# A hybrid conv/mLSTM decoder block on one core: the gates' rows moved by steps, and another order and other engines for the last block's output

## The chip, the cores and the metric

The kernel runs on one core of a Trainium2 chip. The metric is the device time of one execution in microseconds, as the median of several runs. The profile is one further execution, with its own time; the span in it goes from the first to the last instruction.

## What is computed

One decoder block on 512 rows of width 1024 in float32, cut here to what matters:

```python
hn = rmsnorm(x, g_mix)
xa, ba, ca, za, q, k, v, o, zb, ig, fg, ga, gb = split(hn @ w_in)
ya = (ba * causal_short_conv(ca * xa, conv_w, conv_b) * silu(za)) @ w_a_out
hb = mlstm_chunkwise(q, k, v, ig + b_i, fg + b_f)        # 4 heads; log gates, running maximum
yb = (sigmoid(o) * rmsnorm(hb, g_head) * silu(zb)) @ w_b_out
x = x + (sigmoid(ga) * ya + sigmoid(gb) * yb) @ w_o
gate = sigmoid(rmsnorm(x, g_ple) @ w_ple_gate)
x = x + gate * (p @ w_ple)
return rmsnorm(x, g_final)
```

The two input and forget gates are one value per row and head. From them come, per head, cumulative sums, running maxima and the exponents' offsets, here called the gates' rows.

## The kernel before, in words

Every float32 matmul is made of three matmuls on rounded halves: `mm3` (L194 to L198) takes a high half `whi` (rounded on ACT, L144) and a low half `wlo` (what is left, on DVE, L145) of the weights, and two such halves of the other side. `split_half` makes the halves of one half of a weight block, and issues on POOL's queue the loads that add another weight block into the raw one (L151). The raw blocks, four at a time, are loaded over SP's queue (L127).

Most products are `strassen`: seven products of two steps each, a step being twelve matmuls on PE, with the results put together on ACT (`s`, `v`, L307) and DVE (`c`, L311). Its left sides are half-sums of the normalised input, `hs`, rounded by `left` on ACT (L596) and DVE (L598) beside the first such product.

The order of each engine's instructions is that in which the program is written. `step` is called after a step's matmuls and calls `tick`: it resumes the small generators that work beside the matmuls, first the new ones, then makes one piece of a weight split, then resumes the others. A `yield` in a generator is therefore one step of PE. SP's queue alone is ordered by the scheduler.

Around the change three generators matter:

- `gate_rows` (L620 to L679) makes the gates' rows on four partitions, in a tile `rows`: Abs, Exp and Ln on ACT (L629, L630, L636), sums, running maxima and `negm`, `mrow` on DVE (L665, L669). 14 transposes on PE (L674, L676) put them into `ptc`, DVE copies that to `colsb` (L678), ACT makes `enm` (L679). DVE also splits `negm` into `nmr` (L666, L668), which a matmul spreads over the partitions (`pnb`, L744).
- `scores` (L735 on) makes one head's score tiles. Head 0 has its q and k from DRAM: they are loaded into `qk_raw` (L795) once the start's tiles, `rows` among them, are given back, and `cut` (L203, L204) splits them.
- at the end, the product for the gate on `p @ w_ple` is made for columns 0 to 511 in a `block_tm` and for the others by `last_part`, in row blocks t of 128, the last one in two quarters. `gated` takes sigmoid on ACT (L1027), a product and a sum into `xr` on DVE (L1028, L1029) and the sum of squares on ACT (L1030). `power` starts 1/sqrt on POOL, `final` does a Newton step and writes the two halves of the output on DVE (L1064) from `xg`, the product of `xr` and `g_final` that `weighted` made on POOL (L1068); SP issues the stores (L1065).

Of the kernel before, what the change touches and what calls it, by code (L numbers as in the profile page):

```python
# [9 lines left out]
F32 = mybir.dt.float32  # L10
F32R = mybir.dt.float32r
AF = mybir.ActivationFunctionType
ALU = mybir.AluOpType

P = 128
S = 512
NT = S // P
# [19 lines left out]
def hybrid_block(ctx, tc, x, p, g_mix, w_in, conv_w, conv_b, w_a_out, b_gates, g_head,  # L37
# [152 lines left out]
    def drain():  # L190
        while active or fresh:
            tick()
# [55 lines left out]
    def temp(tag, name=None, dt=F32):  # L248

        return tp.tile([P, S], dt, name=name or tag, tag=tag, bufs={"c": 3}.get(tag, 2))  # L250
# [369 lines left out]
    def gate_rows():  # L620
# [3 lines left out]
        yield  # L624
# [6 lines left out]
        yield  # L631
# [13 lines left out]
        yield  # L645
# [20 lines left out]
        dve.tensor_copy(nmr[0:NH], negm)  # L666
        yield
        dve.tensor_tensor(nmr[32:32 + NH], negm, nmr[0:NH].bitcast(F32), ALU.subtract)  # L668
# [6 lines left out]
        for t in range(NT):  # L675
            pe.transpose(ptc[:, 40 + 4 * t:44 + 4 * t], mrow[:, t * P:(t + 1) * P], ident[:NH, :NH])  # L676
        yield
        dve.tensor_copy(colsb, ptc[:, :56])  # L678
        act.activation(enm.rearrange("p t h -> p (t h)"), colsb[:, 40:], AF.Exp)  # L679
# [55 lines left out]
    def scores(h, qk, pr, pp, done, raw):  # L735

        if raw is not None:
            yield
            for m in range(4):
                cut(qk[0][:, m, :], qk[1][:, m, :], raw[:, m, :])  # L740
                if m == 1:
                    yield
# [278 lines left out]
    xg = mp.tile([P, NT, D], F32, name="xg", tag="m")  # L1021

    def gated(ps, t, c, i):

        sl = xr[:, t, c]
        g, sq = (temp(u)[:, :c.stop - c.start] for u in "ec")
        act.activation(g, ps, AF.Sigmoid, scale=er[:, t:t + 1])  # L1027
        dve.tensor_tensor(g, g, ple[:, t, c], ALU.mult)  # L1028
        dve.tensor_tensor(sl, sl, g, ALU.add)  # L1029
        act.activation(sq, sl, AF.Square, accum_out=fss[:, t, i:i + 1])  # L1030

    def gate_embedding(t, ps):
        gated(ps, t, half[0], 0)
        yield

    block_tm([(h2, 0), (h2, HC)], gate_embedding)
    drain()

    base = ep.tile([P, NT], F32, name="base")
    dve.tensor_scalar(base, fss[:, :, 0], 1.0 / D, EPS, ALU.mult, ALU.add)  # L1040
# [10 lines left out]

    def power(t, i):
        a, r, _ = (u[:, t:t + 1] for u in etmp)
        dve.tensor_scalar(a, fss[:, t, i:i + 1], 1.0 / D, base[:, t:t + 1], ALU.mult, ALU.add)
        pool.tensor_tensor(r, a, mhalf[:, :1], ALU.pow)

    def final(t):

        a, r, e = (u[:, t:t + 1] for u in etmp)
        dve.scalar_tensor_tensor(e, r, a, r, ALU.mult, ALU.mult)  # L1060
        dve.tensor_scalar(e, e, -0.5, 1.5, ALU.mult, ALU.add)
        for n in range(2):
            y = temp("sv"[n], "y")
            dve.tensor_scalar(y, xg[:, t, half[n]], r, e, ALU.mult, ALU.mult)  # L1064
            nc.sync.dma_start(out[0, t * P:(t + 1) * P, half[n]], y)  # L1065

    def weighted(t, c):
        pool.tensor_tensor(xg[:, t, c], xr[:, t, c], gfin[:, c], ALU.mult)  # L1068

    pss = [bank(t) for t in range(NT)]  # L1070
    for t in range(2):
        last_part(t, [0], 0, CW, pss[t])
    for t in range(3):
        last_part(t, [1] if t < 2 else [0, 1], 0, CW, pss[t])
# [3 lines left out]
    for t in range(NT):  # L1078
        weighted(t, half[0])
    q = [slice(CW, CW + CW // 2), slice(CW + CW // 2, D)]  # L1080
    gated(pss[0], 0, half[1], 1)
    power(0, 1)
    weighted(0, half[1])
    gated(pss[1], 1, half[1], 1)
    final(0)
    power(1, 1)
    weighted(1, half[1])
    final(1)
    gated(pss[2], 2, half[1], 1)
    power(2, 1)  # L1090
    weighted(2, half[1])
    gated(pss[3][:, :CW // 2], 3, q[0], 1)
    weighted(3, q[0])
    final(2)
    gated(psl[:, :CW // 2], 3, q[1], 2)
    dve.tensor_scalar(base[:, 3:4], fss[:, 3, 1:2], 1.0 / D, base[:, 3:4], ALU.mult, ALU.add)
    weighted(3, q[1])
    power(3, 2)
    final(3)
# [23 lines left out]
```

## Time and profile before

| what | us |
|---|---|
| median of 3 runs | 889.19 (888.02 to 889.53) |
| the profiled execution, its own time | 886.59 |
| its span | 884.8 |
| PE busy | 863.3 (98%) |
| DVE busy | 568.3 (64%) |
| ACT busy | 438.6 (50%) |
| POOL busy | 240.6 (27%) |
| TensorE's mean granted clock | 0.994 of full speed |

The span is shorter than the execution's time by 1.8 us, which lie around it. An engine's busy time is a sum over its instructions; neighbouring ones overlap by up to 0.1 us, so busy time and distance of starts differ a little. A row of the timeline shows in brackets how long the engine had been idle and what ended that. Matmuls overlap: what one costs is the distance of starts.

### The profile page before, as it was taken

The numbers are of one execution on the slowest core, as the hardware profiler recorded it, in microseconds if no ns is written. First come the engines' busy times: TensorE is split into PE (matmuls) and PEld (weight loads), VectorE is DVE, ScalarE is ACT, GpSimd is POOL, SyncE is SP. The second block draws the span as 40 slices with busy tenths as digits, with TensorE's granted clock in tenths as the row PEclk, the third lists the DMA queues.
The fourth block names the chain that finished last, engine by engine and source line by source line (L and its number), as shares of the span: only waits on it lengthen the run. The fifth ranks groups of instructions, "written<-read, shape, count | busy, mean of one in ns | idle before, by whom it ended". The sixth has DMA issues, their size and how long they took to land.

```text
span 884.8 us, 11787 instructions
## 1 busy us (share of the span) xinstructions
PE 863.3 (98%) x4555; PEld 740.3 (84%) x4555; DVE 568.3 (64%) x744; ACT 438.6 (50%) x639; POOL 240.6 (27%) x236
## 2 busy tenths in 40 slices
PE   7999999999999999999999999999999999999995
PEld 6887688888888888888887999999988888888874
DVE  4759586775675667856884678788872323554446
ACT  6477575546545665546575454645431111224442
POOL 4642422332232313223422534243310100000023
PEclk9999999999999999999999999999999999999998
DMA  9799986969846887887869989898996674422002
GB/s 297 252 215 244 253 192 145 234 196 243 206 142 180 198 192 170 237 218 170 216 163 270 236 182 182 181 179 199 210 412 236 199 258 140 134 96 96 0 1 95
DMA packets 97031, 169.64 MB, mean 192 GB/s; under 512 B 6032, under 2 KB 43984, under 8 KB 94544
## 3 DMA queue, kind: packets, MB, share of 16 engines
q0 software_dynamic: 35616, 76.03, 41.2%
q1 hardware_dynamic: 61360, 92.87, 31.9%
q8 instruction: 35, 0.57, 0.3%
q14 instruction: 20, 0.16, 0.1%
HBM read 148.96 MB, written 19.92 MB: 191 GB/s over the span
## 4 chain that ended last, share of the span: by engine, by line
PE 84%; DVE 5%; DMA 4%; ACT 2%; issue 2%; POOL 1%; SPq 0%; POOLq 0%; DVEq 0%; ACTq 0%
PE mm L198 25%; PE mm L197 25%; PE mm L196 25%; DMA wraw<-in_w_in 2%; DVE wlo L145 2%; DMA qk_raw<-qk_d 1%; PE pv L196 1%; PE pv L197 1%; PE pv L198 1%; DVE xr L1029 1%; ACT whi L144 1%; PE ptk L960 1%; PE pty L729 1%; DVE e L1028 1%; DMA pin<-in_p 1%
## 5 line engine op out<-in xcount | busy, mean ns | idle before, releaser
L145 DVE TENSOR_TENSOR wlo<-wraw,whi 128x1024 fp32r<-128x1024 f32 x222 | 283.4, 1281 | 156.5 <-ACT whi L144 155.6
L144 ACT ACTIVATE whi<-wraw 128x1024 fp32r<-128x1024 f32 x224 | 234.5, 1054 | 138.7 <-PE mm L198 98.3
L151 POOL DMA_DIRECT2D wraw<-in_w_in x110 | 138.3, 1446 | 269.5 <-DVE wlo L145 199.1
L196 PE MATMUL mm<-hn_hi,whi 128*128 128x256 f32 (+1 forms) x320 | 105.1, 328 | 0.0
L198 PE MATMUL mm<-hn_hi,wlo 128*128 128x256 f32 (+1 forms) x320 | 104.4, 326 | 0.2 <-POOL wlo L145 0.2
L197 PE MATMUL mm<-hn_lo,whi 128*128 128x256 f32 (+1 forms) x320 | 104.2, 326 | 0.0
L196 PE MATMUL mm<-whi,hs 128*128 128x512 f32 x256 | 100.1, 391 | 0.4 <-ACT v L307 0.3
L197 PE MATMUL mm<-wlo,hs 128*128 128x512 f32 x256 | 99.9, 390 | 0.3 <-DVE wlo L145 0.3
L198 PE MATMUL mm<-whi,hs 128*128 128x512 f32 x256 | 99.7, 389 | 0.0
L307 ACT ACTIVATE s<-mm 128x512 f32<-128x512 f32 x72 | 42.9, 596 | 85.3 <-PE mm L198 85.1
L196 PE MATMUL mm<-whi,hn_hi 128*128 128x512 f32 x192 | 76.2, 397 | 1.0 <-ACT whi L144 0.7
L197 PE MATMUL mm<-wlo,hn_hi 128*128 128x512 f32 x192 | 75.8, 395 | 0.8 <-DVE wlo L145 0.8
L198 PE MATMUL mm<-whi,hn_lo 128*128 128x512 f32 x192 | 75.3, 392 | 0.0
L198 PE MATMUL mm<-hs,wlo 128*128 128x256 f32 x256 | 72.5, 283 | 0.3 <-DVE wlo L145 0.3
L196 PE MATMUL mm<-hs,whi 128*128 128x256 f32 x256 | 72.4, 283 | 0.0
L197 PE MATMUL mm<-hs,whi 128*128 128x256 f32 x256 | 72.4, 283 | 0.0
L198 PEld LDWEIGHTS mm<-hn_hi,wlo 128*128 128x128 f32 x320 | 60.9, 190 | 5.7 <-POOL wlo L145 0.8
L197 PEld LDWEIGHTS mm<-hn_lo,whi 128*128 128x128 f32 x320 | 60.9, 190 | 4.7
L196 PEld LDWEIGHTS mm<-hn_hi,whi 128*128 128x128 f32 x320 | 60.9, 190 | 4.6
L196 PEld LDWEIGHTS mm<-whi,hs 128*128 128x128 f32 x256 | 48.1, 188 | 10.8 <-ACT v L307 0.7
L197 PEld LDWEIGHTS mm<-wlo,hs 128*128 128x128 f32 x256 | 48.1, 188 | 10.3 <-DVE wlo L145 0.8
L198 PEld LDWEIGHTS mm<-whi,hs 128*128 128x128 f32 x256 | 48.1, 188 | 10.0
(257 smaller groups left out, 1662.8 us busy)
## 6 DMA issues: line engine op xcount, KB each, us to landing
wraw<-in_w_in SPq DMA_DIRECT2D x32, 1024.0 KB, 6.3
wraw<-in_w_in POOLq DMA_DIRECT2D x62, 512.0 KB, 7.6
wraw<-in_w_in SPq DMA_DIRECT2D x48, 512.0 KB, 4.8
wraw<-in_w_in POOLq DMA_DIRECT2D x48, 256.0 KB, 5.9
yt_d<-yc POOLq DMA_DIRECT2D x8, 1024.0 KB, 8.4
wraw<-in_w_b_out SPq DMA_DIRECT2D x8, 1024.0 KB, 12.3
yt<-yt_d POOLq DMA_DIRECT2D x8, 1024.0 KB, 10.6
wraw<-in_w_a_out SPq DMA_DIRECT2D x4, 1024.0 KB, 9.8
```

The source lines that it names most:

```text
L144: act.activation(hi, t, AF.Copy)
L145: (e_lo or dve).tensor_tensor(lo, t, hi.bitcast(F32), ALU.subtract)
L151: nc.gpsimd.dma_start(raws[to][:, ks, cs], src[:, ks, :], accum_op=ALU.add)
L196: pe.matmul(ps, lhsT=a[0], rhs=b[0], start=first, stop=False, **kw)
L197: pe.matmul(ps, lhsT=a[0], rhs=b[1], start=False, stop=False, **kw)
L198: pe.matmul(ps, lhsT=a[1], rhs=b[0], start=False, stop=last, **kw)
L307: act.activation(to[i], src, AF.Copy, scale=scale)
L729: pe.transpose(pts[v][:, t * P:(t + 1) * P], y[:, t, v * P:(v + 1) * P], ident)
L960: pe.transpose(pts[k][:, t * P:(t + 1) * P], src[:, t, k * P:(k + 1) * P], ident)
L1028: dve.tensor_tensor(g, g, ple[:, t, c], ALU.mult)
L1029: dve.tensor_tensor(sl, sl, g, ALU.add)
```

## The change

Four yields of `gate_rows` go, and four are put ahead of `enm`, which so stays at its step: every part of the rows comes one to four steps earlier. `mrow` is made with `negm`, a step ahead of the transposes, and the split of `negm` into `nmr` comes behind them. `scores` waits one step more before it cuts head 0's q and k. At the end, the Square and the product with `g_final` of a row block's first half come a step after its sigmoid; the drain stands behind the first two parts of the last block and `base` behind all of them; POOL multiplies only the first half of the columns, the other is multiplied on DVE in the output's own instruction; a new `fs` holds the product of the two factors of the scale; block 2's output stands behind the last sum, and one half of block 3's output is made on ACT.

```diff
--- before.py
+++ after.py
@@ -621,7 +621,6 @@
         for g, dst in enumerate((li, lf)):
             act.activation(dst, psg[64 + 32 * g:64 + 32 * g + NH, :], AF.Identity, bias=bg[:, g:g + 1])
         yield
-        yield
         for g, dst in enumerate((li, lf)):
             dve.tensor_tensor(dst, dst, psg[32 * g:32 * g + NH, :], ALU.add)
         yield
@@ -629,7 +628,6 @@
         act.activation(la, lf, AF.Abs)
         act.activation(la, la, AF.Exp, scale=-1.0)
         yield
-        yield
         dve.tensor_scalar(u1, la, 1.0, None, ALU.add)
         dve.scalar_tensor_tensor(off, u1, 1.0, la, ALU.subtract, ALU.subtract)
         yield
@@ -642,7 +640,6 @@
 
         for t in range(NT):
             dve.tensor_tensor_scan(bc[:, t, :], ones[:NH].broadcast_to([NH, P]), lfv[:, t, :], 0.0, ALU.mult, ALU.add)
-        yield
         dve.tensor_tensor(ul0f, li, bcf, ALU.subtract)
         dve.tensor_copy(ul[:, 0, :], ul0[:, 0, :])
         yield
@@ -663,9 +660,6 @@
             if t % 2:
                 yield
         dve.tensor_scalar(negm, mxf, -1.0, None, ALU.mult)
-        dve.tensor_copy(nmr[0:NH], negm)
-        yield
-        dve.tensor_tensor(nmr[32:32 + NH], negm, nmr[0:NH].bitcast(F32), ALU.subtract)
         dve.tensor_tensor(mrow, negm, bcf, ALU.subtract)
         yield
 
@@ -674,8 +668,12 @@
             pe.transpose(ptc[:, 4 * n:4 * n + 4], ul[:, n, :], ident[:NH, :NH])
         for t in range(NT):
             pe.transpose(ptc[:, 40 + 4 * t:44 + 4 * t], mrow[:, t * P:(t + 1) * P], ident[:NH, :NH])
+        dve.tensor_copy(nmr[0:NH], negm)
+        dve.tensor_tensor(nmr[32:32 + NH], negm, nmr[0:NH].bitcast(F32), ALU.subtract)
         yield
         dve.tensor_copy(colsb, ptc[:, :56])
+        for _ in range(4):
+            yield
         act.activation(enm.rearrange("p t h -> p (t h)"), colsb[:, 40:], AF.Exp)
 
     colsb = const.tile([P, 56], F32, name="colsb")
@@ -735,6 +733,7 @@
     def scores(h, qk, pr, pp, done, raw):
 
         if raw is not None:
+            yield
             yield
             for m in range(4):
                 cut(qk[0][:, m, :], qk[1][:, m, :], raw[:, m, :])
@@ -1018,26 +1017,28 @@
 
     active.append(norm_scale())
     fss = ep.tile([P, NT, 4], F32, name="fss")
-    xg = mp.tile([P, NT, D], F32, name="xg", tag="m")
-
-    def gated(ps, t, c, i):
+    xg = mp.tile([P, NT, D], F32, name="xg", tag="m")[:, :, half[0]]
+
+    def gated(ps, t, c):
 
         sl = xr[:, t, c]
-        g, sq = (temp(u)[:, :c.stop - c.start] for u in "ec")
+        g = temp("e")[:, :c.stop - c.start]
         act.activation(g, ps, AF.Sigmoid, scale=er[:, t:t + 1])
         dve.tensor_tensor(g, g, ple[:, t, c], ALU.mult)
         dve.tensor_tensor(sl, sl, g, ALU.add)
-        act.activation(sq, sl, AF.Square, accum_out=fss[:, t, i:i + 1])
+
+    def squares(t, c, i):
+        act.activation(temp("c")[:, :c.stop - c.start], xr[:, t, c], AF.Square, accum_out=fss[:, t, i:i + 1])
 
     def gate_embedding(t, ps):
-        gated(ps, t, half[0], 0)
-        yield
+        gated(ps, t, half[0])
+        yield
+        squares(t, half[0], 0)
+        pool.tensor_tensor(xg[:, t, :], xr[:, t, half[0]], gfin[:, half[0]], ALU.mult)
 
     block_tm([(h2, 0), (h2, HC)], gate_embedding)
-    drain()
 
     base = ep.tile([P, NT], F32, name="base")
-    dve.tensor_scalar(base, fss[:, :, 0], 1.0 / D, EPS, ALU.mult, ALU.add)
     wl = []
 
     def last_part(t, cs, a, b, ps):
@@ -1049,54 +1050,69 @@
                     [u[kt][:, a:b] for u in wl[c]], c == 0 and kt == 0, c == 1 and kt == HC - 1)
             tick()
 
+    fs = ep.tile([P, NT], F32, name="fs")
+
     def power(t, i):
         a, r, _ = (u[:, t:t + 1] for u in etmp)
         dve.tensor_scalar(a, fss[:, t, i:i + 1], 1.0 / D, base[:, t:t + 1], ALU.mult, ALU.add)
         pool.tensor_tensor(r, a, mhalf[:, :1], ALU.pow)
 
-    def final(t):
-
+    def final_scale(t):
         a, r, e = (u[:, t:t + 1] for u in etmp)
         dve.scalar_tensor_tensor(e, r, a, r, ALU.mult, ALU.mult)
         dve.tensor_scalar(e, e, -0.5, 1.5, ALU.mult, ALU.add)
-        for n in range(2):
-            y = temp("sv"[n], "y")
-            dve.tensor_scalar(y, xg[:, t, half[n]], r, e, ALU.mult, ALU.mult)
-            nc.sync.dma_start(out[0, t * P:(t + 1) * P, half[n]], y)
-
-    def weighted(t, c):
-        pool.tensor_tensor(xg[:, t, c], xr[:, t, c], gfin[:, c], ALU.mult)
+        dve.tensor_tensor(fs[:, t:t + 1], r, e, ALU.mult)
+
+    def final(t, n, on_act=False):
+
+        y = temp("sv"[n], "y")
+        f = fs[:, t:t + 1]
+        if n:
+            dve.scalar_tensor_tensor(y, xr[:, t, half[1]], f, gfin[:, half[1]], ALU.mult, ALU.mult)
+        elif on_act:
+            act.activation(y, xg[:, t, :], AF.Copy, scale=f)
+        else:
+            dve.tensor_scalar(y, xg[:, t, :], f, None, ALU.mult)
+        nc.sync.dma_start(out[0, t * P:(t + 1) * P, half[n]], y)
 
     pss = [bank(t) for t in range(NT)]
     for t in range(2):
         last_part(t, [0], 0, CW, pss[t])
+    drain()
     for t in range(3):
         last_part(t, [1] if t < 2 else [0, 1], 0, CW, pss[t])
     psl = ps_x.tile([P, S], F32, name="mml", tag="x")
     last_part(3, [0, 1], 0, CW // 2, pss[3])
     last_part(3, [0, 1], CW // 2, CW, psl)
-    for t in range(NT):
-        weighted(t, half[0])
+    dve.tensor_scalar(base, fss[:, :, 0], 1.0 / D, EPS, ALU.mult, ALU.add)
     q = [slice(CW, CW + CW // 2), slice(CW + CW // 2, D)]
-    gated(pss[0], 0, half[1], 1)
+    gated(pss[0], 0, half[1])
+    squares(0, half[1], 1)
     power(0, 1)
-    weighted(0, half[1])
-    gated(pss[1], 1, half[1], 1)
-    final(0)
+    gated(pss[1], 1, half[1])
+    squares(1, half[1], 1)
     power(1, 1)
-    weighted(1, half[1])
-    final(1)
-    gated(pss[2], 2, half[1], 1)
+    final_scale(0)
+    for n in range(2):
+        final(0, n)
+    final_scale(1)
+    for n in range(2):
+        final(1, n)
+    gated(pss[2], 2, half[1])
+    squares(2, half[1], 1)
     power(2, 1)
-    weighted(2, half[1])
-    gated(pss[3][:, :CW // 2], 3, q[0], 1)
-    weighted(3, q[0])
-    final(2)
-    gated(psl[:, :CW // 2], 3, q[1], 2)
+    gated(pss[3][:, :CW // 2], 3, q[0])
+    squares(3, q[0], 1)
+    final_scale(2)
+    gated(psl[:, :CW // 2], 3, q[1])
+    squares(3, q[1], 2)
     dve.tensor_scalar(base[:, 3:4], fss[:, 3, 1:2], 1.0 / D, base[:, 3:4], ALU.mult, ALU.add)
-    weighted(3, q[1])
+    final(2, 0)
     power(3, 2)
-    final(3)
+    final(2, 1)
+    final_scale(3)
+    final(3, 0, True)
+    final(3, 1)
     close(ep_ctx, mp_ctx, hp_ctx, tp_ctx, mg_ctx)
```

ACT in the gates' stage, before. `rows` at L629 and L630 are Abs and Exp, at L636 Ln; `whi` are high halves of weights, `hs` those of the left sides, `s` results taken from PSUM:

```order
L596 ACTIVATE hs_116<-hsf_448 128x1024
L307 ACTIVATE s<-mm 128x512
L144 ACTIVATE whi_583<-wraw_336 128x1024
L629 ACTIVATE rows<-rows 4x512
L630 ACTIVATE rows<-rows 4x512
L307 ACTIVATE s<-mm 128x512
L144 ACTIVATE whi_608<-wraw_334 128x1024
L596 ACTIVATE hs_122<-hnf 128x1024
L144 ACTIVATE whi_629<-wraw_334 128x1024
L144 ACTIVATE whi_652<-wraw_440 128x1024
L636 ACT_TABLE_LOAD
L636 ACTIVATE rows<-rows 4x512
```

and now:

```order
L628 ACTIVATE rows<-rows 4x512
L629 ACTIVATE rows<-rows 4x512
L596 ACTIVATE hs_116<-hsf_448 128x1024
L307 ACTIVATE s<-mm 128x512
L144 ACTIVATE whi_585<-wraw_336 128x1024
L307 ACTIVATE s<-mm 128x512
L144 ACTIVATE whi_610<-wraw_334 128x1024
L634 ACT_TABLE_LOAD
L634 ACTIVATE rows<-rows 4x512
L596 ACTIVATE hs_122<-hnf 128x1024
L144 ACTIVATE whi_632<-wraw_334 128x1024
```

Abs, Exp and Ln with its table load stand ahead of more of the high halves; Ln, which was behind `whi_652`, is now ahead of `whi_632`, the second half of the block before.

DVE in the same stage at `negm` (L665 before, L662 now) and `mrow` (L669, L663), before:

```order
L311 TENSOR_TENSOR c<-s,v 128x512
L145 TENSOR_TENSOR wlo_844<-wraw_588,whi_843 128x1024
L665 TENSOR_SCALAR rows<-rows 4x512
L666 CAST nmr<-rows 4x512
L145 TENSOR_TENSOR wlo_868<-wraw_588,whi_867 128x1024
L668 TENSOR_TENSOR nmr<-rows,nmr 4x512
L669 TENSOR_TENSOR rows<-rows 4x512
L678 COPY colsb<-ptc 128x56
```

and now:

```order
L659 SCALAR_TENSOR_TENSOR rows<-rows,carry 4x128
L311 TENSOR_TENSOR c<-s,mm 128x512
L145 TENSOR_TENSOR wlo_776<-wraw_338,whi_775 128x1024
L662 TENSOR_SCALAR rows<-rows 4x512
L663 TENSOR_TENSOR rows<-rows 4x512
L311 TENSOR_TENSOR c<-s,mm 128x512
L145 TENSOR_TENSOR wlo_800<-wraw_334,whi_799 128x1024
L671 CAST nmr<-rows 4x512
L672 TENSOR_TENSOR nmr<-rows,nmr 4x512
L311 TENSOR_TENSOR c<-s,v 128x512
L145 TENSOR_TENSOR wlo_839<-wraw_334,whi_838 128x1024
L674 COPY colsb<-ptc 128x56
```

`mrow` follows `negm` at once, ahead of the casts to `nmr`, and two low halves now stand between `mrow` and the copy of `ptc` to `colsb`.

DVE at the program's end, before (`e` and `xr` of the last quarter are rows 2 and 3):

```order
L1064 TENSOR_SCALAR y<-xg,etmp_6827,etmp_6828 128x512 x2
L1028 TENSOR_TENSOR e<-e,ple 128x256
L1029 TENSOR_TENSOR xr<-xr,e 128x256
L1096 TENSOR_SCALAR base<-fss,base 128x1
L1054 TENSOR_SCALAR etmp_6826<-fss,base 128x1
L1060 SCALAR_TENSOR_TENSOR etmp_6828<-etmp_6827,etmp_6826 128x1
L1061 TENSOR_SCALAR etmp_6828<-etmp_6828 128x1
L1064 TENSOR_SCALAR y<-xg,etmp_6827,etmp_6828 128x512 x2
```

and now:

```order
L1027 TENSOR_TENSOR e<-e,ple 128x256
L1028 TENSOR_TENSOR xr<-xr,e 128x256
L1109 TENSOR_SCALAR base<-fss,base 128x1
L1075 TENSOR_SCALAR y<-xg,fs 128x512
L1057 TENSOR_SCALAR etmp_6826<-fss,base 128x1
L1071 SCALAR_TENSOR_TENSOR y<-xr,fs,gfin 128x512
L1062 SCALAR_TENSOR_TENSOR etmp_6828<-etmp_6827,etmp_6826 128x1
L1063 TENSOR_SCALAR etmp_6828<-etmp_6828 128x1
L1064 TENSOR_TENSOR fs<-etmp_6827,etmp_6828 128x1
L1071 SCALAR_TENSOR_TENSOR y<-xr,fs,gfin 128x512
```

Block 2's output (L1075, L1071) stands behind the last sum, one half of it behind block 3's power input; of block 3's output DVE makes one half.

On PE the 14 transposes stand 36 matmuls earlier, `pnb` twelve later and head 0's score tiles twelve later. On SP three of the four loads of `qk_raw` stand ahead of a weight load that they followed. Nothing else is moved on POOL than the products with `g_final`.

## Rows read from the trace of the kernel before

**Rows 1.** PE's waits, whole span: engine, line, waited for: us, times, longest.

```profile
PE ptc L676 <- DVE rows L669: 1.4, 1, 1.4
```

**Rows 2.** Timeline of PE, 77 to 108: start, us, instruction [idle before <-releaser].

```profile
79.42 0.40 PE L197 MATMUL mm<-wlo,hs 128*128 128x512 f32 x1
...
88.78 0.39 PE L198 MATMUL mm<-whi,hn_lo 128*128 128x512 f32 x1
...
91.65 0.72 PE L196 MATMUL mm<-whi,hn_hi 128*128 128x512 f32 x1
...
95.40 0.40 PE L196 MATMUL mm<-whi,hn_hi 128*128 128x512 f32 x1
...
101.32 0.39 PE L198 MATMUL mm<-whi,hn_lo 128*128 128x512 f32 x1
...
104.89 0.39 PE L196 MATMUL sc<-qk 128*128 128x512 f32 x1
...
107.68 0.50 PE L196 MATMUL mm<-whi,hs 128*128 128x512 f32 x1
```

**Rows 3.** Stages: length, busy time of the five engines, PEclk, DMA share, GB/s.

```profile
92.00:95.00 3.00, 3.00 (x8) 2.32 (x8) 1.23 (x1) 1.16 (x2) 3.00 (x4) 0.50 1.14 253
```

**Rows 4.** Timeline of PE, 856 to 875.

```profile
856.72 0.50 PE L196 MATMUL mm<-whi,h 128*128 128x512 f32 x1 [0.45 <-ACT whi L144]
...
857.98 0.50 PE L197 MATMUL mm<-wlo,h 128*128 128x512 f32 x1 [0.76 <-DVE wlo L145]
...
874.44 0.28 PE L198 MATMUL mml<-whi,h 128*128 128x256 f32 x1
```

**Rows 5.** Timeline of ACT, 50 to 61.

```profile
50.08 1.05 ACT L144 ACTIVATE whi<-wraw 128x1024 fp32r<-128x1024 f32 x1
...
53.75 0.61 ACT L629 ACTIVATE rows<-rows 4x512 f32<-4x512 f32 x1
...
60.84 1.28 ACT L636 ACT_TABLE_LOAD   x1 [0.67 <-DVE rows L634]
```

**Rows 6.** Timeline of DVE, 58 to 78.

```profile
58.50 1.23 DVE L145 TENSOR_TENSOR wlo<-wraw,whi 128x1024 fp32r<-128x1024 f32 x1
...
60.08 0.68 DVE L634 SCALAR_TENSOR_TENSOR rows<-rows 4x512 f32<-4x512 f32 x1
...
67.11 1.22 DVE L145 TENSOR_TENSOR wlo<-wraw,whi 128x1024 fp32r<-128x1024 f32 x1 [3.48 <-ACT whi L144]
...
77.95 1.21 DVE L145 TENSOR_TENSOR wlo<-wraw,whi 128x1024 fp32r<-128x1024 f32 x1
```

**Rows 7.** Stages, DVE's instructions on the tile rows alone: length, busy (count), PEclk, DMA.

```profile
58.40:61.00 2.60, 1.09 (x2) 1.00 1.07 243
...
78.00:88.00 10.00, 3.75 (x14) 1.00 0.77 229
```

**Rows 8.** Timeline of ACT, 876 to 877.

```profile
876.44 0.46 ACT L1027 ACTIVATE e<-mml,er 128x256 f32<-128x256 f32 x1
```

**Rows 9.** Timeline of DVE, 864 to 881.

```profile
864.41 0.69 DVE L1028 TENSOR_TENSOR e<-e,ple 128x512 f32<-128x512 f32 x1 [0.36 <-ACT e L1027]
...
877.40 0.41 DVE L1028 TENSOR_TENSOR e<-e,ple 128x256 f32<-128x256 f32 x1
...
878.90 0.21 DVE L1054 TENSOR_SCALAR etmp<-fss,base 128x1 f32<-128x1 f32 x1 [0.51 <-ACT c L1030]
...
880.22 1.00 DVE L1064 TENSOR_SCALAR y<-xg,etmp,etmp 128x512 f32<-128x512 f32 x2
```

**Rows 10.** SP's stores of the output: line, count: ns min/median/max, first and last start.

```profile
L1065 SPq DMA_DIRECT2D out<-y x8: 332/350/373, 867.7 to 881.2; - x8
```

**Rows 11.** Timeline of DVE and POOL, 261 to 865.

```profile
261.28 1.22 DVE L145 TENSOR_TENSOR wlo<-wraw,whi 128x1024 fp32r<-128x1024 f32 x1
...
261.45 1.96 POOL L865 TENSOR_TENSOR cols<-cols,mhalf 128x4 f32<-128x4 f32 x1 [10.83 <-DVE cols L864]
...
864.19 0.55 POOL L1055 TENSOR_TENSOR etmp<-etmp,mhalf 128x1 f32<-128x1 f32 x1 [7.92 <-DVE etmp L1054]
```

## Prediction

> **What bounds the kernel now.** I read the page first: by its part 1 TensorE is busy nearly throughout, so only what PE waits for, what slows it, and what follows its last matmul can be won. The list of PE's waits puts one of the longest, 1.4 us, on the four transposes L676 that need the row `mrow` [rows 1]. PE's timeline shows what that wait costs: the last matmul before the 14 transposes into `ptc` starts at 88.78, the next one at 91.65; from there to 95.40 nine matmuls start 0.42 us apart, while the 26 that follow to 101.32 start 0.23 apart; and the six matmuls of head 0's first score tile take from 104.89 to 107.68 [rows 2]. The table by stages gives the reason of the slow nine: the clock granted was 0.50, the lower of its two levels, 1.2 of 2.4 GHz [rows 3]. Near the end PE stalls twice, for the high and the low half of the last weight block, and its last matmul starts at 874.44 [rows 4], 10.4 us before the span ends.
>
> The sums stand against one execution: 886.59 us, 884.8 of them span. It lies 2.6 below the median of 889.19 and 1.4 below the fastest of the three runs, so I take differences from it and subtract them from 889.19.
>
> **The change part by part.**
>
> *The wait at ptc.* PE reaches the transposes three steps (36 matmuls) earlier, but `mrow` is made four steps earlier and a whole step ahead of them. From 88.78 to 91.65 is 2.87: 0.23 for the matmul, the rest transposes and wait. The transposes stay. I take −1.4, the listed wait [rows 1]; 0 if `mrow` is late again.
>
> *The clock.* Nine matmuls at 0.42 instead of 0.23 cost 3.75 − 9 × 0.228 = 1.7 us [rows 2]. Without the idle I expect no fall: −1.7, or 0.
>
> *Head 0's scores.* Six matmuls are worth 6 × 0.228 = 1.37 and took 2.79 [rows 2]: PE waited for q and k, which are split as their loads land. The loads wait for the gates' rows, whose space they take; the rows are read out some 7 us earlier, and the splits come a step later. So −1.4, or 0. On SP's queue three of the four loads now stand before one weight load; what they wait for (the last reading of the rows, near 85 by the sum below) ends before that load's buffer comes free (a low half after it), so I cost the move at nothing. The later cut delays `negb` and the scores by one step; the weighted sums that use them come after the whole product for v and o.
>
> *What the earlier rows displace.* This is the price. ACT now does Abs, Exp and an `hs` half ahead of the second weight half. From 50.08, with the durations of the rows and the 0.1 by which ACT's long neighbours overlap (Exp taken as Abs, 0.61, `hs` as a weight half, 1.05), that half starts near 53.75; its low half on DVE ends near 56.0, then come u1 and `off` (0.68), to 57.1. Only then can Ln's table load (1.28) and Ln start, and now they stand ahead of the second half of the third product [rows 5]. That half starts at 60.0, its low half on DVE at 61.0; before it was 58.50 [rows 6]: 2.5 later. From there to the second low half of the sixth product DVE has five low weight halves, three `hs` low halves and two `c` in either order. Before it took 58.50 to 77.95, with 3.48 of idle [rows 6]. The rows' work in the stretch loses u1 and `off` (1.09) and gains what stood in 78 to 88 but for 0.14 of `negm` (3.75 − 0.14 = 3.6) [rows 7]. The idle is used up, so the stretch takes 19.45 − 3.48 − 1.09 + 3.6 = 18.5 and the low half starts at 79.5. It was started at 77.95 and PE read it at 79.42 [rows 2, 6], 0.26 after its end. Now it ends 1.6 later, so PE comes through 1.4 later than before, whichever stalls came in between. **+1.4**. POOL's adds into the raw weights (L151) are issued after the low halves and so come up to 2.5 later; high halves wait for them. The bounds are 0, if DVE catches up, and 2.8, twice the value, which is to cover those adds. `negm` and `mrow` follow (to 81.8); PE reaches the transposes near 82, so `ptc` just finds its row.
>
> The gates' stage together: −1.4 − 1.7 − 1.4 + 1.4 = **−3.1**.
>
> *The last block's splits.* ACT did the Square of row block 3 ahead of both high halves, and it had to wait for DVE's sum. Now one half stands ahead of two Squares and the other ahead of the last. PE loses 0.45 at 856.72, and 1.26 − 0.23 = 1.03 to 857.98 [rows 4]: 1.5. POOL's product with `gfin` and DVE's two-input instructions share time there, which may leave 0.4 of the second stall. POOL's four products keep their place beside PE. I take −1.4, between 1.1 and 1.6.
>
> *The tail.* Before: last matmul 874.44, sigmoid of the last quarter 876.44 because ACT and DVE were behind, power's input `a` 878.90, outputs from 880.22, ended 1.00 later at 881.2, and 3.6 more to the span's end [rows 4, 8, 9]. Now POOL no longer multiplies between DVE's instructions and block 2's output stands behind the last add, so the sigmoid follows the matmul by some 0.35. From sigmoid to `a` were 2.46; the sigmoid ended at 876.90 and DVE, held up in its outputs, took the product at 877.40 [rows 8, 9], so 0.5 of it goes: 2.0. From `a` to the output 1.32, plus 0.2 for the new product `fs`. The two outputs now run side by side, on DVE (a two-input instruction of that size took 0.69 [rows 9]) and on ACT (between the 0.46 of a quarter's 256 columns and the 1.05 of a weight half's 1024 [rows 5, 8]), so 0.7 for both, and one more issue of a store on SP, 0.35 [rows 10], as the two are ready together. Then 3.6. Sum 8.5.
>
> To it comes a hold. `final(2, 1)` now reads two tiles on DVE and starts while the last power waits to start. At 261.28 such a DVE instruction ran 1.22; the power that POOL took up at 261.45 needed 1.96 and ended 0.9 after it, where a power of one column takes 0.55 [rows 11]. I add 0.6: 9.1 against 10.4, **−1.3**. The bounds are −1.9, with no hold, and −1.2, with the 0.7 of a whole output. By the Trainium skill, "SBUF — State Buffer", section "SBUF: two separate sides", the pair of ports is locked for a whole instruction and the loser blocks, in either direction. The trace agrees for the power behind DVE; it does not for DVE behind a power: the product at 864.41 began inside the power of 864.19 and took its usual 0.69 [rows 9, 11]. By the rule the last power is held and the sum stays; had no lock been at work, it would be 882.8.
>
> Sum: −3.1 − 1.4 − 1.3 = −5.8, so **883.4 us**.
>
> **The rivals.**
>
> *The rows cost PE nothing* (0.17): DVE finishes in time, as its idle of 3.48 suggests. Against it: the sum of 18.5 has no idle left. −7.2: 882.0.
>
> *The clock falls all the same* (0.13): the new stall of about 1.4 and the transposes that follow within two microseconds may do what wait and transposes did. For it: the rows at 91.65 [rows 2, 3]; against it: the two stalls at 856.72 were not followed by slow matmuls. −5.8 + 1.7: 885.1. The Trainium skill's "TensorE: Matmul & The Clock Gate", Part 1, has the clock follow how busy the array has been lately, which allows it.
>
> *The change doesn't do what it says* (0.09): DVE is later than I sum, `mrow` is late at the transposes, PE idles and the clock falls as before. Then only −1.4 of q and k, −1.4 and −1.3 are left, less the 1.4 of the late half: −2.7, 886.5.
>
> *Slower* (0.06): the late low halves stall PE at each product of the stage, and each stall lets the clock fall. One fall costs 1.7. It turns the sign when 5.8 / 1.7 = 3.4 falls come, and is seen as slower with 4.5; with five, one per product touched, 883.4 + 8.5 = 891.9. Against it: PE's waits of this size elsewhere show no fall.
>
> **How the numbers follow.** The forecast has 0.55. Its best bounds (no displaced time, 1.6 and 1.9 at the end) give −4.5 − 1.6 − 1.9 = −8.0, 881.2, and 0.9 of spread below, as the runs lie up to 1.2 apart: 880.3. Its worst (2.8 displaced, the clock falling, 1.1 and 1.2) give −1.4 − 1.4 + 2.8 − 1.1 − 1.2 = −2.3: 886.9. With the third rival inside and the slower one out, 880.3 to 887.0. A measurement tells about 0.2%, 1.8 us, from no change: faster means under 887.4. All cases but the slower one lie there; since displaced work may be larger than I see, 0.87 faster, 0.08 same, 0.05 slower.
>
> **What would show it.** No wait of `ptc` on `mrow`; a granted clock of full speed behind the transposes; score tile 0 in 1.4 us. A stall of PE on a low half near 79.5 to 81, in the stage's sixth product. No stall on the last weight block, and the last matmul some 4.5 us earlier. A last power of 1.0 to 1.2 instead of 0.55. The forecast is wrong if PE waits more than 3 us in the gates' stage, or if the clock falls there.

## The result and the profile after

The changed kernel takes 882.03 us in the median of 6 runs (880.89 to 883.67), the kernel before 888.51 in the 6 runs beside it: a ratio of 0.9932 (95% interval 0.9916 to 0.9948), which is 6.0 us less; the two medians lie 6.5 apart. The prediction of 883.4 stood against a median of 889.19, a difference of 5.8. So it was right in sign and size; a second comparison in 5 rounds (below) gave 0.9931 (0.9917 to 0.9946). The two profiled executions lie only 5.0 apart, because that of the kernel before was 1.9 faster than the median of its runs and that of the changed kernel 0.5.

| what | before | after |
|---|---|---|
| the profiled execution, its own time | 886.59 | 881.56 |
| its span | 884.8 | 879.8 |
| PE busy | 863.3 | 861.4 |
| DVE busy | 568.3 | 568.6 |
| ACT busy | 438.6 | 439.1 |
| POOL busy | 240.6 | 236.6 |
| mean granted clock | 0.994 | 0.997 |

The list of PE's waits after (engine, line, waited for: us in total, times, longest) has no `ptc` any more. The low halves read at L197 stand in second place as before; their longest wait is now 1.0, where it was 0.8.

```profile
PE ptp L468 <- DMA pin<-in_p: 4.9, 2, 3.7
PE mm L197 <- DVE wlo L145: 1.7, 2, 1.0
PE mm L196 <- ACT whi L144: 0.9, 1, 0.9
PE mm L198 <- DVE wlo L145: 0.7, 1, 0.7
...
PE pty L727 <- DVE gty L859: 0.2, 1, 0.2
```

PE's timeline after, from the gates' stage to the end, answers to [rows 2, 4]:

```profile
80.77 0.50 PE L197 MATMUL mm<-wlo,hs 128*128 128x512 f32 x1 [0.98 <-DVE wlo L145]
...
82.13 0.78 PE L668 MATMUL ptc<-ident,rows 4*128 4x4 f32 x10
82.77 0.39 PE L670 MATMUL ptc<-ident,rows 4*128 4x4 f32 x4
83.09 0.50 PE L196 MATMUL mm<-whi,hs 128*128 128x512 f32 x1
...
105.62 0.39 PE L196 MATMUL sc<-qk 128*128 128x512 f32 x1
...
106.98 0.39 PE L196 MATMUL mm<-whi,hs 128*128 128x512 f32 x1
...
854.16 0.39 PE L196 MATMUL mm<-whi,h 128*128 128x512 f32 x1
854.38 0.39 PE L197 MATMUL mm<-wlo,h 128*128 128x512 f32 x1
...
870.67 0.28 PE L198 MATMUL mml<-whi,h 128*128 128x256 f32 x1
```

And DVE's, for the low half that PE waits for and for `mrow`:

```profile
79.51 1.21 DVE L145 TENSOR_TENSOR wlo<-wraw,whi 128x1024 fp32r<-128x1024 f32 x1
...
81.09 0.68 DVE L663 TENSOR_TENSOR rows<-rows 4x512 f32<-4x512 f32 x1
```

Each step of the forecast can be read here. The second low half of the sixth product starts at 79.51 (forecast 79.5) and its matmul at 80.77 instead of 79.42: 1.35 later. `mrow` ends at 81.77, the last four transposes start at 82.77 without a wait, and the matmul after them 0.32 later. Score tile 0 takes 106.98 − 105.62 = 1.36. The two stalls on the last weight block are gone. The stage table (length, busy time of the five engines, PEclk, DMA share, GB/s) shows the full clock both behind the transposes and where it was 0.50 before [rows 3]:

```profile
83.00:86.00 3.00, 3.00 (x16) 2.48 (x16) 2.93 (x5) 1.36 (x2) 0.57 (x1) 1.00 1.00 388
92.00:95.00 3.00, 3.00 (x15) 2.48 (x14) 0.30 (x1) 2.97 (x5) 3.00 (x5) 1.00 1.08 291
```

The same matmuls compared one by one: those of the first weighted sums (one at 140.45 before, at 137.37 after) start 3.08 earlier. In the middle 1.13 of that is lost, so that at 836.97 only 1.95 is left; the last block wins 1.82, and the tail, from the start of the last matmul to the end of the span, shrinks from 10.39 to 9.12. −3.08 + 1.13 − 1.82 − 1.27 = −5.0, the difference of the spans. The 1.13 was in no one's sum.

### The profile page after: what moved, and what is told of

The parts are those of the page before. It is cut to its first block, busy times and chain, and to the rows that moved or that the text cites. A ratio compares the mean times of both kernels' runs of the same rounds, so it can differ in the third digit from the quotient of the medians.

```text
span 879.8 us, 11790 instructions
## 1 busy us (share of the span) xinstructions
PE 861.4 (98%) x4555; PEld 739.6 (84%) x4555; DVE 568.6 (65%) x747; ACT 439.1 (50%) x640; POOL 236.6 (27%) x231
## 4 chain that ended last, share of the span: by engine, by line
PE 84%; DVE 5%; DMA 5%; issue 3%; ACT 2%; POOL 1%; SPq 0%; POOLq 0%; DVEq 0%; ACTq 0%
PE mm L198 25%; PE mm L197 25%; PE mm L196 25%; DMA wraw<-in_w_in 4%; DVE wlo L145 2%; ACT whi L144 1%; PE pv L196 1%; PE pv L197 1%; PE pv L198 1%; PE ptk L959 1%; PE pty L727 1%; DMA pin<-in_p 0%; DMA z_d<-c 0%; PE sc L198 0%; PE sc L197 0%
## 5 line engine op out<-in xcount | busy, mean ns | idle before, releaser
L197 PE MATMUL mm<-hn_lo,whi 128*128 128x256 f32 (+1 forms) x320 | 104.2, 326 | 0.0
L197 PE MATMUL mm<-wlo,hs 128*128 128x512 f32 x256 | 100.2, 391 | 1.3 <-DVE wlo L145 1.0
L197 PE MATMUL mm<-wlo,hn_hi 128*128 128x512 f32 x192 | 75.0, 391 | 0.8 <-DVE wlo L145 0.8
L197 PE MATMUL mm<-hs,whi 128*128 128x256 f32 x256 | 72.4, 283 | 0.0
L197 PEld LDWEIGHTS mm<-hn_lo,whi 128*128 128x128 f32 x320 | 60.9, 190 | 4.7
L197 PEld LDWEIGHTS mm<-wlo,hs 128*128 128x128 f32 x256 | 48.1, 188 | 12.4 <-DVE wlo L145 3.0
```

The source lines that it names most:

```text
L197: pe.matmul(ps, lhsT=a[0], rhs=b[1], start=False, stop=False, **kw)
```

## The experiments

To set traces side by side, the table gives how much later (+) the same matmuls start than in the trace of before: the median over those that lay within 5 us behind the place named, less the same median over 40 to 60. The places are times in the trace of before: 96.5 lies behind the transposes into `ptc`, 122 behind the first score tiles, 141 at the first weighted sums, 505 behind the middle, 862 in the last block. The value over 40 to 60, the start, differs from execution to execution because PE waits for its first loads. The tail is the span less the start of the last matmul.

| trace | start | 96.5 | 122 | 141 | 505 | 862 | tail |
|---|---|---|---|---|---|---|---|
| before | 0 | 0 | 0 | 0 | 0 | 0 | 10.4 |
| before_again | +0.05 | +0.03 | +0.34 | +0.35 | +1.22 | +1.22 | 10.4 |
| mrow_first | −0.47 | −3.17 | −0.59 | −0.59 | −0.04 | −0.07 | 10.4 |
| end_only | −0.01 | −1.60 | +1.46 | +1.46 | +1.64 | −0.18 | 9.1 |
| gates_only | +0.62 | −0.53 | −2.09 | −2.09 | −1.46 | −1.47 | 10.4 |
| changed kernel | +0.07 | −2.06 | −3.62 | −3.15 | −2.02 | −3.83 | 9.1 |
| after_again | −0.11 | −2.06 | −3.62 | −3.49 | −2.40 | −4.22 | 9.1 |
| after_5 | +0.79 | −0.50 | −2.06 | −2.06 | −0.99 | −2.81 | 9.1 |
| rows_one_later | +0.83 | −3.31 | −4.26 | −3.40 | −2.09 | −3.91 | 9.1 |
| cut_at_old_step | −0.04 | −2.07 | −3.63 | −3.08 | −2.52 | −4.34 | 9.1 |
| square_at_once | +0.24 | −2.05 | −3.62 | −3.37 | −2.74 | −2.74 | 9.1 |
| tail_two_first | +0.39 | −2.05 | −3.61 | −3.23 | −2.34 | −4.16 | 8.7 |
| tail_two_first_5 | −0.40 | −2.05 | −3.61 | −3.42 | −1.77 | −3.59 | 8.7 |
| three_together | +0.13 | −3.25 | −3.29 | −2.49 | −1.77 | −3.60 | 8.8 |

### The two halves of the change by themselves

gates_only is the kernel before with the hunks on `gate_rows` and `scores`; end_only is the kernel before with all the others.

> The kernel before with the moved gates' rows and the later cut of head 0's q and k, and with the old end. By the sum, the first weighted sum of head 0 starts 3.1 us earlier than the 140.45 of before (137.4), with a new stall of PE on a low half near 80.8, and the last block loses 1.5 to its two halves as before, so the whole is 3.1 less by the profile. But the changed kernel's trace gives 1.1 of that back between 375 and 497. If the give-back belongs to the gates' part, the last matmul comes 1.9 to 2.0 earlier than 874.44 (872.5); if it belongs to the end's part, 3.1 earlier (871.4). The tail stays at 10.4.

> The kernel before with the new end alone. Up to 850 nothing should move: the first weighted sum at 140.4, the matmul after the low half at 498.8. The two stalls at 856.7 and 858.0 go: the last matmul 1.4 to 1.8 earlier than 874.44 (872.6 to 873.0), and the span ends 9.1 after it instead of 10.4, the last power taking 1.0 instead of 0.55. Together 2.7 to 3.1 less. Rival: the give-back of 1.1 in the middle comes with the end's part (other places of the tiles); then the matmul of 498.8 comes about 1.1 later and only 1.6 to 2.0 are left.

gates_only: 0.9962 (0.9951 to 0.9972) of before; end_only: 0.9964 (0.9952 to 0.9977). Their product, 0.9926, is the whole change's ratio within its interval: the two halves do not disturb each other by more than can be measured. end_only has the last block (from +1.64 to −0.18, so −1.82) and the tail (9.1) of the changed kernel. The give-back belongs to neither: between 141 and 505 gates_only loses 0.6 and end_only 0.2.

Both profiles showed something that was not expected, though, and it is the clock. gates_only is 1.5 behind the changed kernel at 96.5 with the same instructions up to there; what differs is that its matmuls right behind the transposes ran at the low clock. So its last matmul came at 873.58, later than either expectation. end_only, which has the gates' code of before, did not fall to the low clock behind `ptc` (1.60 earlier at 96.5), although PE waited there as long as in before [rows 1]. But then it waited longer for head 0's q and k and fell behind those waits, and its last matmul came at 874.25 instead of the expected 872.6 to 873.0. PE in end_only:

```profile
91.31 0.41 PE L676 MATMUL ptc<-ident,rows 4*128 4x4 f32 x4 [1.44 <-DVE rows L669]
...
104.47 0.50 PE L196 MATMUL sc<-qk 128*128 128x512 f32 x1 [1.02 <-ACT qk L203]
...
105.81 0.50 PE L198 MATMUL sc<-qk 128*128 128x512 f32 x1 [0.61 <-DVE qk L204]
...
108.37 0.63 PE L197 MATMUL mm<-wlo,hs 128*128 128x512 f32 x1
108.80 0.63 PE L198 MATMUL mm<-whi,hs 128*128 128x512 f32 x1
```

and two stages of it, in the columns of the stage table above:

```profile
92.00:95.00 3.00, 3.00 (x15) 2.47 (x14) 1.23 (x1) 1.41 (x3) 3.00 (x4) 1.00 1.09 249
...
108.00:111.00 3.00, 3.00 (x8) 2.38 (x9) 2.06 (x3) 1.50 (x5) 1.20 (x1) 0.55 1.09 283
```

Score tile 0 started 0.42 earlier than in before [rows 2] although PE was 1.6 ahead: q and k set that time, and PE's lead goes into waiting for them. The matmul behind the tile starts at 107.78, where it started at 107.68 before: all of the lead of 1.6 is gone there, and the low clock behind it cost most of the 1.46 that the table has at 122.

### mrow first, no step moved

```diff
+        dve.tensor_tensor(mrow, negm, bcf, ALU.subtract)
         dve.tensor_copy(nmr[0:NH], negm)
         yield
         dve.tensor_tensor(nmr[32:32 + NH], negm, nmr[0:NH].bitcast(F32), ALU.subtract)
-        dve.tensor_tensor(mrow, negm, bcf, ALU.subtract)
         yield
```

> The kernel before with mrow made straight after negm, ahead of both instructions for nmr; no step is moved. mrow should end near 89.0 instead of 91.3, so the last four transposes wait for nothing (1.4 less), and if the low clock behind them came from that idle time, the nine slow matmuls run at 0.23 (1.7 less): pnb 3.1 earlier than 101.64. Then two theories part. If the terms add up, the first weighted sum starts 3.1 earlier than 140.45. If the wait at head 0's scores is set by the landing of q and k, whose loads still start near 91 since their space is read until then, PE only waits longer there: the third matmul of score tile 0 stays near 105.7 and the first weighted sum comes less than 0.7 earlier.

This is the cleanest test of the first three terms of the sum. The wait and the nine slow matmuls went: −3.17 at 96.5, as forecast (−1.4 − 1.7). But at 122 only 0.59 is left. The third matmul of score tile 0, expected near 105.7, came at 104.15: 1.05 earlier than in before when the earlier start of this execution is taken off. PE in mrow_first:

```profile
88.64 0.79 PE L674 MATMUL ptc<-ident,rows 4*128 4x4 f32 x10
89.29 0.39 PE L676 MATMUL ptc<-ident,rows 4*128 4x4 f32 x4
89.61 0.50 PE L196 MATMUL mm<-whi,hn_hi 128*128 128x512 f32 x1
...
102.80 0.50 PE L196 MATMUL sc<-qk 128*128 128x512 f32 x1 [1.39 <-ACT qk L203]
...
104.15 0.79 PE L198 MATMUL sc<-qk 128*128 128x512 f32 x1 [0.61 <-DVE qk L204]
```

PE ran into q and k, waited 1.39 and 0.61, and then fell to the low clock (104.15 to 107.00) as well. The theory that the terms simply add up falls here; the one that the landing of q and k sets the scores stands. But the 2.6 that go between 96.5 and 122 are not all the loads': the seven matmuls from 104.15 on took 1.65 longer than at 0.23 apiece, and this run does not tell how much of that PE would have waited for q and k at the full clock. The loads can start only when the rows' space is given back, and that is what the four steps buy. Before, the last instructions that read the rows are PE's transposes from 91.32 on, which end at 91.73; in the changed kernel it is the split of `negm`, which ends at 84.56. The first load follows on SP's queue, 0.02 and 0.07 behind. SP in before, then DVE and SP in the changed kernel:

```profile
91.75 3.10 SPq L795 DMA_DIRECT2D qk_raw<-qk_d  x4
```

```profile
83.88 0.68 DVE L672 TENSOR_TENSOR nmr<-rows,nmr 4x512 fp32r<-4x512 f32 x1
```

```profile
84.63 1.29 SPq L794 DMA_DIRECT2D qk_raw<-qk_d  x3
```

In mrow_first, where the split of `negm` is the last reader too, the first load is issued at 90.78, only 0.5 earlier than in before when the start is taken off.

### The later cut of q and k

```diff
         if raw is not None:
             yield
-            yield
             for m in range(4):
```

> The changed kernel without the later cut: head 0's q and k are split one step earlier, as far behind the start of the scores as before. If the gain at the scores comes from the loads, which now start near 84.6 instead of 91.75, PE waits for q and k no more than in the changed kernel (no idle listed at score tile 0) and the weighted sum marked at 137.37 keeps its place within 0.3, or comes earlier since DVE's splits of the scores then lie a step further from the low half that PE waits for at 125. If the later cut is what took the wait away, PE waits for q and k again, by up to 1.4.

No wait at score tile 0, and the same places at 122 (−3.63 against −3.62) and 141 (−3.08 against −3.15 to −3.49): the later cut is worth at most 0.4. The 1.4 comes from the earlier loads.

### The displaced rows' work

```diff
             if t % 2:
                 yield
+            if t == 1:
+                yield
...
-        for _ in range(4):
+        for _ in range(3):
             yield
```

> The changed kernel with one yield more between the running maxima of t = 1 and t = 2, and one less ahead of enm: the rows come three steps earlier than before from there on instead of four, so 1.24 us of scans stand behind the sixth product's second low half instead of ahead of it. If the displaced rows' work is what costs 1.35 there, the low half starts near 78.3 instead of 79.51, PE's wait of 0.98 at 80.77 goes and the first weighted sum starts near 136.1 instead of 137.37. Rivals: the stall only moves on to the next low half or to the transposes (mrow ends near 83.2, PE comes there near 83.5), and the weighted sum stays at 137.4; or q and k, loaded some 2 us later than now, come late and take it back.

In DVE's timeline of rows_one_later the low half now stands ahead of the scans:

```profile
79.02 1.21 DVE L145 TENSOR_TENSOR wlo<-wraw,whi 128x1024 fp32r<-128x1024 f32 x1
80.16 0.14 DVE L657 TENSOR_TENSOR carry<-rows 4x1 f32<-4x1 f32 x1
```

Less the later start of this execution (0.76) it began at 78.26, as expected, and PE's wait went: −3.31 at 96.5, 1.25 better than the changed kernel. So the term of +1.4 was rightly sized and rightly placed. It is not to be had, though: at 141 only −3.40 is left, within what the changed kernel's own executions reach (−3.15 to −3.49). Part is lost behind 101, part at 125, where PE waits 0.57 for a low half that DVE starts late. In the changed kernel too a low half at 119.27 takes 2.79 where others take 1.21, beside two adds of POOL (DVE, then POOL):

```profile
119.27 2.79 DVE L145 TENSOR_TENSOR wlo<-wraw,whi 128x1024 fp32r<-128x1024 f32 x1
```

```profile
119.47 3.18 POOL L772 TENSOR_TENSOR pp<-pp 128x384 f32<-128x384 f32 x2
```

three_together joins this edit with the earlier cut and the shorter tail (below):

> Three edits of the changed kernel together: the scans of t = 2 and 3 one step later, head 0's q and k cut at the old step, and the two-input half of block 2's output ahead of the last power with the other half on ACT. The first alone took PE's wait at 80.8 away and got back 1.3 by 99, but lost it to waits behind 101 and at 125. If DVE's load around 119 to 126 is what took it back, it is relieved by the earlier cut and up to 1.3 stays at the weighted sums (136.1 against a start like that of the changed kernel); with the tail's 0.4 the span would be 878.1 to 879.4. Rival: q and k, loaded later in this version, land after the earlier cut and PE waits for them; then nothing is won but the tail's 0.4.

It failed: −3.29 at 122 and −2.49 at 141. No wait for q and k, but three on weight halves, at 118.31 (0.18), 119.57 (0.76) and 125.82 (0.50). I read this as the scores' splits and DVE's low halves falling together, which was not tested by itself. Only the tail's 0.4 came.

### What comes again: both kernels unchanged

> The kernel before, unchanged, to see what of its trace comes again. Theory one, that the low clock belongs to the idle at ptc: nine matmuls behind the transposes at 0.42 as before, and PE's wait of 0.28 at 498.8. Theory two, after end_only, where the same gates' code ran the matmuls behind ptc at 0.23 and fell to the low clock only behind q and k's waits at 108.4 to 110.5: the fall has no fixed place; it comes once, at ptc or at the scores, and costs 1.4 to 1.8 in either. On the give-back: if 0.28 at 498.8 was the exception (0.75 to 0.76 in all five other traces), it is 0.75 here as well.

> The changed kernel, unchanged, to see what of its trace comes again. Fixed: the wait of 0.98 on the low half near 80.8 and none at 856 to 858, the tail of 9.1. Open: the clock. gates_only, the same code up to here, fell to the low clock behind the transposes (83.7 to 87.1, some 1.6 lost), the trace of the changed kernel did not. If the fall is excluded by the change, it is absent here; if it is only less likely, it may come, and the first weighted sum then starts near 138.9 instead of 137.4.

> The changed kernel, timed in the same rounds. Ratio 0.9925 to 0.994 to the kernel before; in its profile the wait of 0.98 on the low half near 80.8, no low clock behind the transposes and a tail of 9.1.

before_again fell to the low clock behind `ptc` again. after_again did not; after_5 did. Its stage in the columns above:

```profile
83.00:86.00 3.00, 3.00 (x19) 2.60 (x19) 2.93 (x6) 2.06 (x3) 0.57 (x1) 0.62 0.87 315
```

With the same wait of 0.99 ahead of it and the same transposes, this execution lost 1.56 there (−0.50 against −2.06 at 96.5), of which 1.1 to 1.4 are left at 141. Over all traces: each of the four without the moved steps fell once, two at `ptc` and two behind q and k's waits. Of the ten with them eight did not fall and two did (gates_only and after_5), both behind the transposes. So the change makes the fall rarer (two of ten against four of four); it does not exclude it.

The give-back: in all traces but the first of before PE waits 0.75 or 0.76 for a low half near 498. In before:

```profile
498.76 0.39 PE L198 MATMUL mm<-hs,wlo 128*128 128x256 f32 x1 [0.28 <-DVE wlo L145]
```

in before_again:

```profile
500.02 0.38 PE L198 MATMUL mm<-hs,wlo 128*128 128x256 f32 x1 [0.76 <-DVE wlo L145]
```

That trace of before was a lucky one there: 0.47 of the 1.13 lost in the middle is the longer wait here. Another 0.4 goes at PE's wait for `gty` in the list of waits after, where three of the ten traces with the moved steps lose 0.2 to 0.4 and none of the four without. From 141 to 505 the four traces without the moved steps lose 0 to 0.9 (mean 0.4), the ten with them 0.6 to 1.7 (mean 1.0). A loss of about half a microsecond may be the change's own; the executions lie too far apart to say. The wait itself goes back to a high half that stands idle for a weight load, 2.98 in before and 3.45 to 4.04 in the thirteen others; in the changed kernel:

```profile
494.43 2.01 ACT L144 ACTIVATE whi<-wraw 128x1024 fp32r<-128x1024 f32 x2 [3.45 <-DMA wraw<-in_w_in]
```

### The Square at the last block

```diff
         gated(ps, t, half[0])
+        squares(t, half[0], 0)
         yield
-        squares(t, half[0], 0)
```

> The changed kernel with the Square of a row block's first half straight behind its sigmoid again, everything else as changed. If it was ACT's wait for DVE's sum, ahead of both high halves of the last weight block, that stalled PE at 856.7 and 858.0, both stalls come back (0.45 and 0.76 as listed, 1.5 to 1.8 in the distance of starts) and the last matmul comes 1.5 to 1.8 later than in the changed kernel, against the matmuls at 840. If the move of the drain or of POOL's products did it, PE does not stall.

Both stalls came back, to the hundredth as in [rows 4], and with them 1.81: against the changed kernel PE goes there from 0.55 ahead to 1.26 behind, while the drain and POOL's products stayed where the change put them. PE in square_at_once:

```profile
854.22 0.50 PE L196 MATMUL mm<-whi,h 128*128 128x512 f32 x1 [0.45 <-ACT whi L144]
855.47 0.50 PE L197 MATMUL mm<-wlo,h 128*128 128x512 f32 x1 [0.76 <-DVE wlo L145]
```

So this gain is ACT's order alone.

### The tail

```diff
-    final(2, 0)
-    power(3, 2)
     final(2, 1)
+    power(3, 2)
+    final(2, 0, True)
```

> The changed kernel with the two-input half of block 2's output ahead of the last power's input and the other half on ACT, so that DVE runs nothing beside the last power. If the power is held by the two-input output on DVE, it takes 0.55 instead of 0.98; its input comes 0.1 to 0.2 later, so the scale of block 3 comes 0.3 to 0.5 earlier and the span ends 8.6 to 8.8 behind the last matmul instead of 9.13. Rival: the 0.98 comes from POOL standing idle for 3.8 us before it; then it stays 0.98 and the tail grows to 9.2 or 9.3.

> The changed kernel with the shorter tail of tail_two_first, timed side by side with the changed kernel and with the kernel before. By the profiles it ends 0.4 earlier than the changed kernel, so 6.5 to 7 less than before (a ratio near 0.992); 0.4 is 0.05%, which the intervals will hardly part from the changed kernel. In the profile the last power takes 0.54 again and the tail 8.7. Rival: the 0.4 was one execution's luck; then the tail is 9.1.

The end of the changed kernel, ACT at the last quarter's sigmoid, then DVE, then POOL:

```profile
870.99 0.47 ACT L1026 ACTIVATE e<-mml,er 128x256 f32<-128x256 f32 x1 [0.43 <-PE mml L198]
```

```profile
873.01 0.21 DVE L1057 TENSOR_SCALAR etmp<-fss,base 128x1 f32<-128x1 f32 x1
873.14 0.74 DVE L1071 SCALAR_TENSOR_TENSOR y<-xr,fs,gfin 128x512 f32<-128x512 f32 x1
874.32 0.22 DVE L1062 SCALAR_TENSOR_TENSOR etmp<-etmp,etmp 128x1 f32<-128x1 f32 x1 [0.43 <-POOL etmp L1058]
```

```profile
873.30 0.98 POOL L1058 TENSOR_TENSOR etmp<-etmp,mhalf 128x1 f32<-128x1 f32 x1 [3.77 <-DVE etmp L1057]
```

and of tail_two_first, DVE, then POOL:

```profile
872.42 0.74 DVE L1071 SCALAR_TENSOR_TENSOR y<-xr,fs,gfin 128x512 f32<-128x512 f32 x1
873.08 0.20 DVE L1057 TENSOR_SCALAR etmp<-fss,base 128x1 f32<-128x1 f32 x1
873.94 0.22 DVE L1062 SCALAR_TENSOR_TENSOR etmp<-etmp,etmp 128x1 f32<-128x1 f32 x1 [0.66 <-POOL etmp L1058]
```

```profile
873.36 0.54 POOL L1058 TENSOR_TENSOR etmp<-etmp,mhalf 128x1 f32<-128x1 f32 x1 [3.84 <-DVE etmp L1057]
```

The hold is shown: with nothing on DVE beside it the power takes 0.54, after the same idle time, and the tail is 8.74 instead of 9.12. This version was timed in 5 rounds beside the changed kernel: 0.9926 (0.9914 to 0.9939) of before, median 881.2, against 0.9931 and 882.08. The profiles give it 0.4 us; the timing does not tell the two apart.

## Why the prediction was right, step by step

- **The wait at `ptc`, −1.4**: right. 81.81 to 83.09 are 1.28 where there were 2.87, so 1.6.
- **The clock, −1.7**: right in eight of ten executions; in two the rival came true that the clock falls all the same, at the place it named (the stall and the transposes behind it), for about 1.55. One of them, after_5, is the changed kernel itself: by the prediction's own last sentence it was wrong in that execution. With a fall in one execution of five its share of the sum is 0.3.
- **Head 0's scores, −1.4**: the size was right (score tile 0 in 1.36 us, an advance from −2.06 to −3.62), the reason half right. It is the earlier loads that count, not the later cut. And the three terms were put down as if each stood alone. mrow_first shows that they do not: without the earlier loads the first two are worth 0.6 together, since PE then waits for q and k instead, and the clock falls behind that wait. The sum came out because the change has all of them.
- **The displaced work, +1.4**: 1.35, at the low half and the time named. What the step did not see is that taking it away would bring next to nothing, because DVE's low halves at 119 to 126 come next.
- **The gates' stage, −3.1**: −3.08 in the first trace, or −3.15 with its start taken off; the others with the same gates' steps and no low clock have −3.1 to −3.5.
- **The last block, −1.4**: 1.81 to 1.82, so the cause was right and the size 0.4 too small. The 1.5 it starts from counts the first stall by its listed idle time of 0.45, where the distance of starts (855.88 to 856.72, less 0.23) is 0.61, and leaves out the matmul behind the second, which starts 0.34 later and not 0.23. Another 0.1 was taken off for POOL beside DVE. That contention is there (below): it delays DVE's products and draws the two low halves out, from 2.36 to 3.46 for both, but the high halves no longer wait for those products, and PE reads both low halves without a stall.
- **The tail, −1.3**: −1.27. The sigmoid of the last quarter follows the last matmul by 0.32 (forecast 0.35, before 2.0), the power's input follows the sigmoid by 2.02 (forecast 2.0). The hold was put at 0.6 and is 0.44.
- **Not in the sum**: the 1.13 lost in the middle. The range of 880.3 to 887.0 held because it was reckoned from the ends of the terms and the spread of the runs; the loss, had it been seen, would have moved the forecast up by half a microsecond or so, about as much as the last block was undersized. That the two cancel, and that 883.4 lies within 1.4 of the measured median, is in part luck.

## What to carry to other kernels

A stall that is removed is worth only what the next wait behind it leaves, and that wait may be a load that can start only when the space of the late data itself is given back: price the steps of a chain together, and test the first one alone. An instruction that waits for another engine should not stand ahead of the halves that PE needs, even if it is itself on no critical path. And one profile of before is one draw: a repetition of the unchanged kernel showed which of its waits were its own.

## What the runs showed of the hardware

- **The clock.** The same instructions behind the same wait (0.95 to 0.99) kept the full clock in six executions of eight and fell to the lower level in two, for 1.5 to 1.6 us each time. In the code of before, the wait of 1.43 or 1.44 at `ptc` brought the fall in two executions and not in end_only, which came to it within 0.02 us of the time of before. The two of the eight that fell had also started latest (0.62 and 0.79, the others 0.39 at most). rows_one_later started as late (0.83) and did not fall, but there PE had no such wait, so it does not settle whether the start matters. The chip alone does not decide: after_5 fell and tail_two_first_5, on the same one, did not. What decides stays open. The Trainium skill's "TensorE: Matmul & The Clock Gate", Part 1, ties the level to how busy the array was lately; the falls agree, as all of them came behind waits of PE, but no run here shows why the same wait gives both.
- **DVE beside POOL.** At the last block DVE's products take 1.39 to 1.54 instead of the 0.69 of before [rows 9]; each begins inside one of POOL's products and ends 0.54 to 0.55 behind its end (DVE, then POOL, changed kernel):

```profile
844.20 1.54 DVE L1027 TENSOR_TENSOR e<-e,ple 128x512 f32<-128x512 f32 x1 [0.17 <-ACT e L1026]
846.92 1.46 DVE L1027 TENSOR_TENSOR e<-e,ple 128x512 f32<-128x512 f32 x1 [0.46 <-ACT e L1026]
849.64 1.39 DVE L1027 TENSOR_TENSOR e<-e,ple 128x512 f32<-128x512 f32 x1 [0.53 <-ACT e L1026]
```

```profile
843.22 1.97 POOL L1037 TENSOR_TENSOR xg<-xr,gfin 128x512 f32<-128x512 f32 x1 [11.60 <-DVE xr L1028]
846.54 1.29 POOL L1037 TENSOR_TENSOR xg<-xr,gfin 128x512 f32<-128x512 f32 x1 [1.36 <-DVE xr L1028]
849.19 1.30 POOL L1037 TENSOR_TENSOR xg<-xr,gfin 128x512 f32<-128x512 f32 x1 [1.35 <-DVE xr L1028]
```

  A power of one column did not do that to the product at 864.41 [rows 9, 11]. By these rows the whole-size POOL product holds DVE, and by the tail's experiment DVE's two-input output holds the one-column power. The Trainium skill's "SBUF — State Buffer", section "SBUF: two separate sides", lets the one that begins first keep the shared ports for its whole instruction. These rows agree, in both directions; the low half at 119.27, which began ahead of POOL's adds and still took 2.79, does not, as far as POOL's rough spans tell.
